# Depthwise convolution taps: from VectorE and GpSimd to VectorE and float32 products on TensorE

## The chip, the cores and the metric

The kernel runs on one core of a Trainium2 chip. The metric is the device time of one execution in microseconds; the time of a kernel is the median of its runs. The engines are named as in the profile: PE is TensorE's matrix products (PEld its weight loads), DVE is VectorE, ACT is ScalarE, POOL is GpSimd.

## The reference

Two decoder layers on 256 tokens of width 1024. In each layer one normalised input feeds two groups: attention with three branches, and a convolution module on 512 channels. Their outputs go through one output projection; a dense (layer 0) or a routed (layer 1) channel mixer follows. The convolution module is what the change is about:

```python
CONV_WIDTH = D_MODEL // 2      # 512 channels
CONV_KERNEL = 31               # taps
...
def conformer_conv(u, conv_w, conv_b, ln_g, ln_b):
    a, g = jnp.split(u, 2, axis=-1)
    h = a * jax.nn.sigmoid(g)
    h = jnp.pad(h, ((0, 0), (CONV_KERNEL - 1, 0), (0, 0)))
    y = lax.conv_general_dilated(h, conv_w[:, None, :], window_strides=(1,), padding='VALID',
                                 dimension_numbers=('NWC', 'WIO', 'NWC'),
                                 feature_group_count=CONV_WIDTH)
    y = y + conv_b
    return jax.nn.silu(layer_norm(y, ln_g, ln_b))
```

Each channel has its own 31 weights, so the convolution is 31 shifted copies of `h`, each times one number per channel, summed.

## The kernel before

Weights stream from memory in tiles of 1 MB; each half tile is split into two float32r parts, `wh` on ScalarE (line 189) and `wl` on VectorE (line 190), and each product with weights is three float32r products (`mm3`, lines 275 to 277). Inside a layer's attention phase nothing is scheduled by a planner: the string `SEQ` is a list of unit names, and the program issues the units in that order. Each engine runs its own instructions strictly in that order and waits at an instruction until what it needs from other engines is there.

The convolution is channel-major: four chunks of 128 channels (two *pairs* of chunks), 256 tokens along a row. The units that matter here:

- `uA` and `uB` are the input projections of pair 0 and pair 1, 16 units each, six products of 256 columns a unit. After the last unit of a pair, `glu` writes the gated input of the pair to `hpad` (ScalarE `th`, VectorE `hpad`).
- `v` is one tap of one chunk on VectorE (`tap_v`, line 593): `cv = cv + hpad shifted * weight`, 128 x 256. The first 17 taps of pair 0 and 16 of pair 1 go this way (`NDT`), 66 units a layer.
- `g` is one tap of one chunk in two steps (`tap_g`): ScalarE multiplies (`tap`, line 602), GpSimd adds to `cvg` (line 603). These are the other 14 and 15 taps, 58 units a layer.
- `S0` to `S11` are the score steps of attention: products into `pss` (lines 699 and 702), then VectorE's row minimum `nm` (line 704), then ScalarE's exponentials `sc` (line 707). `P0` to `P11` transpose a step's exponentials on TensorE (`ptp`, line 844) and copy them out on ScalarE (`prT`, line 846). `V0` to `V11` are the float32 products with the values (`po`, line 859).
- `ph0` to `ph3` are float32 products of 31 columns for the compressed branch (line 774), `gelu`, `heads`, `cnorm` and `keys` what follows on them; `cs`, `cp`, `cv0`, `cv1` are the compressed branch's scores (`psc`, line 867, then `scmp` on VectorE and `pcmp` on ScalarE), probabilities and values.
- `lm0` and `lm1` add `cvg` to `cv` (line 925), `lmean` begins the layer norm over channels with float32 products `pmean` of 256 columns (line 930).

The accumulation tiles of two banks each (`acc_bank`) rotate over two buffers: `pkv`, `pu` of pair 0, `pu` of pair 1, `po` of both token blocks, `pout`.

Of the kernel before, what the change touches and what calls it, by code (L numbers as in the profile page):

```python
# [47 lines left out]
NDT = (17, 16)  # L48
NPT = (0, 0)
SEQ = """  # L50
    qr0 kv kv qs1 qr1 kv kv kv kv qx1 kv kv qs0 ks1 kvc kvc kvc kvc kvc kvc qt11 kr0 kr1 ks0 kvc kvc uA uA uA
    setup uA uA gt gt gt kx0 uA uA uA kx1 gt qx0 uA uA uA kt10 uA uA uA uA uA v kvo gt kt00 v gt v g v g g g v v v
    v g v swap blk1 g v blk0 uB g g v gt uB v v g v uB g kt01 kt11 uB uB g gt v uB qt10 g uB v uB v g v gtan v g v
    uB uB v uB v g g v v v qt00 g uB qt01 g g uB g g g S0 ph0 g v uB ph1 gate v g v g v S1 v v v ph2 uB v v uB g
    P0 ph3 v g P1 gelu v g S2 heads v g g g v g P2 S3 S4 cnorm V0 g v v V1 v keys v g S5 v g P3 cs0 v g g v V2 g
    P4 S6 P5 v v v g V3 S7 v cs1 g g v cp0 g g S8 g v V4 P6 g g P7 g g join0 S9 cv0 cp1 v V5 v g g V6 v turn0 g g
    v v v lm0 g V7 oa g P8 g g P9 S10 S11 g V8 v v oa P10 g P11 v v v v V9 v V10 v v lm1 V11 join1 lmean cv1 oa
# [12 lines left out]
def trunk(ctx: ExitStack, tc: tile.TileContext, x, positions, attn_norm_g, ffn_norm_g, w_in, w_out,  # L70
# [28 lines left out]
    # ------------------------------------------------------------------ the stream of weights  # L99
# [49 lines left out]
    class Stream:  # L149
        """Weight tiles in the order of use: loads run RAW tiles ahead, the split into two  # L150
        float32r parts runs WB - 1 half tiles ahead."""
# [21 lines left out]
        def whole(self):  # L173
            """the next tile that is used as it is, and its number"""
            n = self.order[1].pop(0)
            return n, self.raws[n]
# [29 lines left out]
        def take_group(self, n):  # L206
            """n parts of one half tile each that are used more than once: no half tile beyond
            the buffers is split before their use"""
            return [self.take(WB - j) for j in range(n)]
# [9 lines left out]
    # ------------------------------------------------------------------ first loads  # L219
# [17 lines left out]
    # ------------------------------------------------------------------ constants  # L237
# [100 lines left out]
    def boundary(key, nrm, tails, heads, banks, **more):  # L338
        """the end of one part and the start of the next, with the norm between them; the order is
        that of the letters: o, a unit of the end (the last four those of the second token block);  # L340
        h, a unit of the start for the first block; z y x and a q u t, the norm of the two blocks;
        m, half a weight tile to split"""
# [7 lines left out]
    # ------------------------------------------------------------------ rest of the setup  # L350
# [103 lines left out]
    def rope(sm, v, cs, sn):  # L454
        """v [n, heads, 64]; the first 16 of the last axis rotated in place"""
# [11 lines left out]
    # ================================================================== layers  # L467
    for layer in range(DEPTH):
# [16 lines left out]
        # ---- queries, token-major  # L485
# [70 lines left out]
        # ---- inputs of the convolution, channel-major: two chunks of 128 channels at a time  # L556
# [18 lines left out]
        cvg = nsm.tile([P, D], F32, name="cvg", tag="xn").rearrange("p (c t) -> p c t", c=4)  # L575
# [9 lines left out]
        # causal depthwise conv, tap by tap beside other work: the first taps of a chunk on VectorE,  # L585
        # some on TensorE, the others multiplied on ScalarE and summed on GpSimd
# [9 lines left out]
        def tap_g(c, j, first):  # L596
            src = hpad[:, c, j:j + S]
            if first:
                nc.scalar.activation(cvg[:, c], src, AF.Copy, scale=cw5[layer][:, c, j:j + 1])
            else:  # L600
                tap = sm.tile([P, S], F32, name="tap", bufs=3)
                nc.scalar.activation(tap, src, AF.Copy, scale=cw5[layer][:, c, j:j + 1])  # L602
                nc.gpsimd.tensor_tensor(cvg[:, c], cvg[:, c], tap, op=ALU.add)  # L603

        pcv = {}

        def tap_p(pair, j, first, last):
            """a tap of two chunks on TensorE, by diagonal matrices"""
            cs_ = slice(2 * pair, 2 * pair + 2)
            if first:  # L610
                pcv[pair] = bank_a("pcv").rearrange("p (c t) -> p c t", c=2)
            dg = sm.tile([P, 2, P], F32, name="dg", tag="tap", bufs=3)
            nc.gpsimd.tensor_tensor(dg, ident[:, None, :].to_broadcast([P, 2, P]),
                                    cw5[layer][:, cs_, j:j + 1].to_broadcast([P, 2, P]), op=ALU.mult)
            for c in range(2):
                nc.tensor.matmul(pcv[pair][:, c], dg[:, c], hpad[:, 2 * pair + c, j:j + S],
                                 start=(first and c == 0), stop=last, skip_group_check=True)

        vs, gs, ps = [], [], []
        for pair in range(2):  # L620
            nd = NDT[pair]
            ng = nd + NPT[pair]
            vs.append([lambda c=c, j=j: tap_v(c, j) for j in range(nd) for c in (2 * pair, 2 * pair + 1)])
            ps.append([lambda pair=pair, j=j, nd=nd, ng=ng: tap_p(pair, j, j == nd, j == ng - 1)
                       for j in range(nd, ng)])
            gs.append([lambda c=c, j=j, ng=ng: tap_g(c, j, j == ng) for j in range(ng, CONV_K)
                       for c in (2 * pair, 2 * pair + 1)])

        def some(lst, n):
            for _ in range(n):  # L630
                for pair in sorted(ready):
                    if lst[pair]:
                        lst[pair].pop(0)()
                        break
# [6 lines left out]
        # ---- keys and values of the causal branches: token-major  # L641
# [41 lines left out]
        # ---- attention: the two causal branches, 512 score columns a step; the steps of both  # L683
        # token blocks form one pipeline
# [26 lines left out]
        # ---- inputs of the compressed branch and gates, channel-major  # L711
# [50 lines left out]
        # ---- compressed keys and values  # L762
# [74 lines left out]
        # ---- the steps of attention after the scores  # L837
# [79 lines left out]
        # ---- layer norm of the conv over channels and swish  # L917
        ln = {}

        def ln_merge(pair):  # L920
            c = slice(2 * pair, 2 * pair + 2)
            if NPT[pair]:
                nc.vector.tensor_tensor(cv[:, c], cv[:, c], pcv[pair], op=ALU.add)
            if NDT[pair] + NPT[pair] < CONV_K:
                nc.vector.tensor_tensor(cv[:, c], cv[:, c], cvg[:, c], op=ALU.add)
# [44 lines left out]
        # ---- output projection  # L970
# [17 lines left out]
        def out_conv(k, b):  # L988
            if b == 0 and k == 0:
# [11 lines left out]
                 "p": [lambda: some(ps, 1)] * (2 * CONV_K),  # L1001
                 "v": [lambda: some(vs, 1)] * (4 * CONV_K), "g": [lambda: some(gs, 1)] * (4 * CONV_K),
# [21 lines left out]
        events += [("lm0", lambda: ln_merge(0)), ("lm1", lambda: ln_merge(1)), ("lmean", ln_mean), ("lvar", ln_var), ("lscale", ln_scale), ("lout", ln_out)]  # L1024
# [6 lines left out]
        for name in SEQ.split():  # L1031
            units[name].pop(0)()
        phase.close()

        # ---- channel mixer
# [5 lines left out]
        # the scale of the tokens is left out where the experts apply it  # L1041
# [9 lines left out]
        def logits(b):  # L1051
            """the router's logits of a token block, channel-major"""
# [14 lines left out]
        if layer % 2 == 0:  # L1067
# [44 lines left out]
            def ffn_first():  # L1112
                """the first columns, token-major: the first token block starts before the second"""
# [70 lines left out]
        # ---- routed experts  # L1184
# [10 lines left out]
        # rank of each logit in its row; equal logits rank by index  # L1195
# [12 lines left out]
        # slot of each token within its expert: tokens before it that chose the same expert  # L1208
# [24 lines left out]
        def gather(pair, banks):  # L1233
            """the tokens of a pair of experts, channel-major; in units of 256 channels and one part"""
# [33 lines left out]
        def of_slots(dst, ps, e, src):  # L1268
            """a value of each token, for the tokens in the slots of an expert"""
# [271 lines left out]
```

## Time and profile before

| | |
|---|---|
| time, median of 3 runs | 1623.56 us (1615.91 to 1625.65) |
| span of the profiled execution, first to last instruction | 1617.5 us |
| PE busy over the span | 1546.0 us (96%) |
| DVE busy | 1342.1 us (83%) |
| ACT busy | 1093.4 us (68%) |
| POOL busy | 126.0 us (8%) |
| mean granted TensorE clock | 0.971 |

The span is the only time that the profiled execution has of itself; it lies 6 us under the median of the runs and inside their range. A granted clock of 1.0 is 2.4 GHz, 0.5 is 1.2 GHz; a mean between them is a share of both. Busy shares are averages over the program: the attention phase of layer 0 takes roughly the first 160 us, that of layer 1 lies between 412 and 560 us, and in the rest of the time the mixers run with PE over 90% busy and GpSimd idle. Durations of single instructions overlap with those of their neighbours, so a row that merges several (x7) gives the better price of one.

### The profile page before, as it was taken

What the parts mean: (1) busy time and instruction counts of PE and PEld (TensorE: products, weight loads), DVE (VectorE), ACT (ScalarE), POOL (GpSimd) and SP (SyncE); (2) the same over time, 40 slices, a digit from 0 to 9 for tenths busy, and PEclk for the clock granted to TensorE, in tenths of its full rate; (3) what the DMA queues carried; (4) which work ended last, traced back from release to release, by engine and by line L of the source; (5) the groups of instructions that cost most, each with busy time, mean ns of one, the idle gap of its engine ahead of it and who ended that gap; (6) DMA issues with size and microseconds to landing.
All of it is one profiled execution on the core that took longest, in us unless ns stands there. A gap on an engine that the chain in (4) does not pass through costs nothing.

```text
span 1617.5 us, 21390 instructions
## 1 busy us (share of the span) xinstructions
PE 1546.0 (96%) x7861; PEld 1294.0 (80%) x7861; DVE 1342.1 (83%) x1647; ACT 1093.4 (68%) x1430; POOL 126.0 (8%) x152
## 2 busy tenths in 40 slices
PE   6989999999997989999999999999999999999997
PEld 5977899999796768878877877887877877878785
DVE  7898655554789889989989989989989989998995
ACT  5765544444466568777877877777877777777774
POOL 2453000000155200000000000000000000000000
PEclk9978999999997999999999999999999999999998
DMA  9700585546632249999999998999999999998990
GB/s 307 223 27 1 187 304 182 183 167 198 158 105 79 79 151 373 378 323 335 362 336 337 371 337 314 359 349 338 371 339 330 338 353 329 367 369 314 362 364 27
DMA packets 197744, 433.75 MB, mean 268 GB/s; under 512 B 10346, under 2 KB 28978, under 8 KB 197636
## 3 DMA queue, kind: packets, MB, share of 16 engines
q1 hardware_dynamic: 196902, 432.02, 75.6%
q8 instruction: 63, 1.03, 0.3%
q0 software_dynamic: 288, 0.30, 0.1%
q14 instruction: 45, 0.37, 0.1%
q10 hardware_dynamic: 446, 0.03, 0.0%
HBM read 431.27 MB, written 1.05 MB: 267 GB/s over the span
## 4 chain that ended last, share of the span: by engine, by line
PE 77%; DVE 17%; ACT 3%; issue 2%; DMA 1%; POOL 0%; SPq 0%; DVEq 0%; ACTq 0%
PE pg L275 12%; PE pg L277 12%; PE pg L276 12%; PE pd L277 7%; PE pd L276 7%; PE pd L275 7%; DVE wl L190 5%; DVE cv L593 4%; PE pgu L275 3%; PE pgu L277 3%; PE pgu L276 3%; PE pt L288 2%; ACT wh L189 1%; PE pgx L1243 1%; DVE xt L1404 1%
## 5 line engine op out<-in xcount | busy, mean ns | idle before, releaser
L190 DVE TENSOR_TENSOR wl<-raw,wh 128x1024 fp32r<-128x1024 f32 x808 | 981.3, 1227 | 189.3 <-ACT wh L189 164.7
L189 ACT CAST wh<-raw 128x1024 fp32r<-128x1024 f32 x808 | 845.9, 1052 | 326.7 <-PE pg L277 126.4
L275 PE MATMUL pg<-wh,xgH 128*128 128x512 f32 x896 | 353.8, 395 | 6.5 <-DVE xt L1404 6.5
L277 PE MATMUL pg<-wh,xgL 128*128 128x512 f32 x896 | 353.5, 394 | 0.0
L276 PE MATMUL pg<-wl,xgH 128*128 128x512 f32 x896 | 352.5, 393 | 0.0
L275 PE MATMUL pd<-wh,fh 128*128 128x512 f32 x560 | 226.5, 404 | 0.1
L276 PE MATMUL pd<-wl,fh 128*128 128x512 f32 x560 | 222.2, 397 | 1.3 <-DVE wl L190 1.3
L277 PE MATMUL pd<-wh,fl 128*128 128x512 f32 x560 | 222.9, 398 | 0.0
L275 PEld LDWEIGHTS pg<-wh,xgH 128*128 128x128 f32 x896 | 170.3, 190 | 43.8 <-ACT wh L189 9.3
L277 PEld LDWEIGHTS pg<-wh,xgL 128*128 128x128 f32 x896 | 169.9, 190 | 36.5 <-DVE xgL L1247 0.5
L276 PEld LDWEIGHTS pg<-wl,xgH 128*128 128x128 f32 x896 | 170.5, 190 | 35.8 <-DVE wl L190 0.3
L276 PEld LDWEIGHTS pd<-wl,fh 128*128 128x128 f32 x560 | 105.8, 189 | 24.9 <-DVE wl L190 2.0
L277 PEld LDWEIGHTS pd<-wh,fl 128*128 128x128 f32 x560 | 105.6, 189 | 25.1 <-DVE fl L272 0.2
L275 PEld LDWEIGHTS pd<-wh,fh 128*128 128x128 f32 x560 | 105.9, 189 | 22.8 <-ACT fh L271 0.3
L275 PE MATMUL pgu<-hFH,wh 128*128 128x256 f32 x384 | 108.9, 284 | 0.8 <-DVE posT L452 0.8
L277 PE MATMUL pgu<-hFH,wl 128*128 128x256 f32 x384 | 108.7, 283 | 0.0
L276 PE MATMUL pgu<-hFL,wh 128*128 128x256 f32 x384 | 108.7, 283 | 0.0
L603 POOL TENSOR_TENSOR cvg<-cvg,tap 128x256 f32<-128x256 f32 x108 | 97.4, 929 | 75.4 <-ACT tap L602 71.9
L275 PEld LDWEIGHTS pgu<-hFH,wh 128*128 128x128 f32 x384 | 73.7, 192 | 1.1 <-PE pgk L1080 0.9
L276 PEld LDWEIGHTS pgu<-hFL,wh 128*128 128x128 f32 x384 | 73.7, 192 | 0.2
L277 PEld LDWEIGHTS pgu<-hFH,wl 128*128 128x128 f32 x384 | 73.7, 192 | 0.0
L593 DVE SCALAR_TENSOR_TENSOR cv<-hpad,cw,cv 128x256 f32<-128x256 f32 x124 | 72.2, 635 | 0.0
(371 smaller groups left out, 1655.1 us busy)
## 6 DMA issues: line engine op xcount, KB each, us to landing
raw<-in_moe_w_gate_dram SPq DMA_DIRECT2D x112, 1024.0 KB, 5.5
raw<-in_moe_w_up_dram SPq DMA_DIRECT2D x112, 1024.0 KB, 5.7
raw<-in_moe_w_down_dram SPq DMA_DIRECT2D x112, 1024.0 KB, 5.1
raw<-in_w_in_dram SPq DMA_DIRECT2D x18, 1024.0 KB, 9.5
raw<-in_ffn_w_gate_dram SPq DMA_DIRECT2D x14, 1024.0 KB, 7.9
raw<-in_ffn_w_up_dram SPq DMA_DIRECT2D x14, 1024.0 KB, 5.1
raw<-in_ffn_w_down_dram SPq DMA_DIRECT2D x14, 1024.0 KB, 4.9
raw<-in_w_out_dram SPq DMA_DIRECT2D x8, 1024.0 KB, 10.6
```

The source lines that it names most:

```text
L189: nc.scalar.copy(h, r)
L190: nc.vector.tensor_tensor(lo, r, h.bitcast(F32), op=ALU.subtract)
L275: nc.tensor.matmul(dst, ah, bh, start=start, stop=False, skip_group_check=skip)
L276: nc.tensor.matmul(dst, ah, bl, start=False, stop=False, skip_group_check=skip)
L277: nc.tensor.matmul(dst, al, bh, start=False, stop=stop, skip_group_check=skip)
L288: nc.tensor.transpose(pt[:, k], src[:, k * P:(k + 1) * P], ident)
L593: nc.vector.scalar_tensor_tensor(cv[:, c], src, cw5[layer][:, c, j:j + 1], cv[:, c], op0=ALU.mult, op1=ALU.add)
L603: nc.gpsimd.tensor_tensor(cvg[:, c], cvg[:, c], tap, op=ALU.add)
L1243: nc.tensor.matmul(pgx, src[:, b, k * P:(k + 1) * P], ohs[pair][:, b].rearrange("p e s -> p (e s)"), start=(m == 0 and b == 0), stop=(m == ...
L1404: nc.vector.tensor_tensor(xt[:, b, ns], xt[:, b, ns], pc, op=ALU.add)
```

## The change

`NDT` becomes 19 for both pairs. The other 12 taps of a chunk are made on TensorE, by a unit `p`: for one tap of one pair, ScalarE writes two diagonal matrices `dg` (the identity, 128 x 128, times the tap's weights as scale), and TensorE multiplies each as float32 with the shifted `hpad` (128 x 256) into `pcv`, an accumulation tile of two banks from `acc_bank`. There are 24 units `p` a layer, 48 products, with three buffers for `dg`. All `g` units are gone, with `cvg`; GpSimd has no part in the convolution. `lp0` and `lp1` add `pcv` to `cv` and stand right after `cs1`; further `v` units follow them. `SEQ` is rewritten accordingly. The core of the diff (blanked comments are left out):

```diff
-NDT = (17, 16)
-NPT = (0, 0)
+NDT = (19, 19)
 SEQ = """
     qr0 kv kv qs1 qr1 kv kv kv kv qx1 kv kv qs0 ks1 kvc kvc kvc kvc kvc kvc qt11 kr0 kr1 ks0 kvc kvc uA uA uA
-    setup uA uA gt gt gt kx0 uA uA uA kx1 gt qx0 uA uA uA kt10 uA uA uA uA uA v kvo gt kt00 v gt v g v g g g v v v
-    v g v swap blk1 g v blk0 uB g g v gt uB v v g v uB g kt01 kt11 uB uB g gt v uB qt10 g uB v uB v g v gtan v g v
-    uB uB v uB v g g v v v qt00 g uB qt01 g g uB g g g S0 ph0 g v uB ph1 gate v g v g v S1 v v v ph2 uB v v uB g
-    P0 ph3 v g P1 gelu v g S2 heads v g g g v g P2 S3 S4 cnorm V0 g v v V1 v keys v g S5 v g P3 cs0 v g g v V2 g
-    P4 S6 P5 v v v g V3 S7 v cs1 g g v cp0 g g S8 g v V4 P6 g g P7 g g join0 S9 cv0 cp1 v V5 v g g V6 v turn0 g g
-    v v v lm0 g V7 oa g P8 g g P9 S10 S11 g V8 v v oa P10 g P11 v v v v V9 v V10 v v lm1 V11 join1 lmean cv1 oa
+    setup uA uA gt gt gt kx0 uA uA uA kx1 gt qx0 uA uA uA kt10 uA uA uA uA uA v kvo gt kt00 v gt v v v v v
+    v swap blk1 v v blk0 uB gt uB v v v v uB kt01 kt11 uB uB v gt v uB qt10 v uB v uB v v gtan v v
+    uB uB v uB v v v v v qt00 uB qt01 p uB p S0 ph0 p v v uB ph1 gate p v p v S1 p v v v ph2 uB p v v uB
+    p P0 ph3 v p v P1 gelu p v S2 heads p v v p v P2 p S3 p S4 p cnorm V0 p v v V1 p v keys p v S5 v p P3 p cs0 v p v V2
+    P4 p S6 P5 v v v p V3 p S7 v cs1 lp0 lp1 cp0 S8 v V4 P6 v P7 join0 S9 cv0 cp1 v V5 v v V6 v turn0
+    v v v v v v V7 oa v P8 P9 S10 S11 V8 v v oa P10 P11 v v v v V9 v V10 v v V11 join1 lmean cv1 oa
     lvar turn1 lscale oa oa lout oa oa oa
 """
...
-        cvg = nsm.tile([P, D], F32, name="cvg", tag="xn").rearrange("p (c t) -> p c t", c=4)
...
-        def tap_g(c, j, first):
-            src = hpad[:, c, j:j + S]
-            if first:
-                nc.scalar.activation(cvg[:, c], src, AF.Copy, scale=cw5[layer][:, c, j:j + 1])
-            else:
-                tap = sm.tile([P, S], F32, name="tap", bufs=3)
-                nc.scalar.activation(tap, src, AF.Copy, scale=cw5[layer][:, c, j:j + 1])
-                nc.gpsimd.tensor_tensor(cvg[:, c], cvg[:, c], tap, op=ALU.add)
-
...
+        def tap_p(pair, j):
+            if not pcv:
+                pcv["p"] = acc_bank("pcv").rearrange("p a (c t) -> p a c t", c=2)
+            dg = sm.tile([P, 2, P], F32, name="dg", bufs=3)
             for c in range(2):
+                nc.scalar.activation(dg[:, c], ident, AF.Copy, scale=cw5[layer][:, 2 * pair + c, j:j + 1])
+            for c in range(2):
+                nc.tensor.matmul(pcv["p"][:, pair, c], dg[:, c], hpad[:, 2 * pair + c, j:j + S],
+                                 start=(j == NDT[pair] and c == 0), stop=(j == CONV_K - 1), skip_group_check=True)
...
-            if NPT[pair]:
-                nc.vector.tensor_tensor(cv[:, c], cv[:, c], pcv[pair], op=ALU.add)
-            if NDT[pair] + NPT[pair] < CONV_K:
-                nc.vector.tensor_tensor(cv[:, c], cv[:, c], cvg[:, c], op=ALU.add)
+            assert not ps[pair]
+            nc.vector.tensor_tensor(cv[:, c], cv[:, c], pcv["p"][:, pair], op=ALU.add)
```

On TensorE the score steps S3 and S4 of layer 0 and the first value products stood in a row before (`pss` S3, `pss` S4, `po` V0 and V1, `pkc` the keys, `pss` S5); line numbers are those of the kernel before:

```order
L844 MATMUL ptp<-ident,sc_1155 128x128 x4
L699 MATMUL pss<-kT,qT 128x256 x4
L702 MATMUL pss<-cmask,identR 128x512
L699 MATMUL pss<-kT,qT 128x512 x2
L702 MATMUL pss<-cmask,identR 128x2x128
L859 MATMUL po<-v_sb,prT 128x64 x8
L833 MATMUL pkc<-ident,kcd 128x16 x2
L699 MATMUL pss<-kT,qT 128x512 x2
```

The same place on TensorE in the changed kernel, whose lines 825, 680, 683 and 840 are the transposes, the two score lines and the value products, and whose line 604 is the new product:

```order
L825 MATMUL ptp<-ident,sc_1129 128x128 x4
L604 MATMUL pcv<-hpad,dg 128x256 x2
L680 MATMUL pss<-kT,qT 128x256 x4
L683 MATMUL pss<-cmask,identR 128x512
L604 MATMUL pcv<-hpad,dg 128x256 x2
L680 MATMUL pss<-kT,qT 128x512 x2
L683 MATMUL pss<-cmask,identR 128x2x128
L604 MATMUL pcv<-hpad,dg 128x256 x2
L840 MATMUL po<-v_sb,prT 128x64 x4
L604 MATMUL pcv<-hpad,dg 128x256 x2
```

A unit `p`, two products, now stands between the transposes and S3, between S3 and S4, and behind S4.

On ScalarE the same place before, where `sc` are the exponentials of S3 and of S4, `tap` and `cvg` the multiplied taps, and `prT` the copy of P2:

```order
L602 ACTIVATE tap<-hpad,cw_604 128x256 [waits Pool_49] x2
L846 COPY prT<-ptp 128x512 [waits PE_49]
L707 ACTIVATE sc_1202,rsum<-pss,nm 128x128 [waits DVE_49]
L707 ACTIVATE sc_1202,rsum<-pss,nm 128x128 x3
L707 ACTIVATE sc_1215,rsum<-pss,nm 128x256 [waits DVE_49]
L707 ACTIVATE sc_1215,rsum<-pss,nm 128x256
L602 ACTIVATE tap<-hpad,cw_604 128x256 [waits Pool_49]
```

And on ScalarE in the changed kernel, whose lines 827, 688 and 602 are the copy, the exponentials and the diagonal matrices:

```order
L827 COPY prT<-ptp 128x512 [waits PE_49]
L602 ACTIVATE dg<-ident,cw_603 128x128 [waits Activation_49]
L602 ACTIVATE dg<-ident,cw_603 128x128
L688 ACTIVATE sc_1184,rsum<-pss,nm 128x128 [waits DVE_49]
L688 ACTIVATE sc_1184,rsum<-pss,nm 128x128 x3
L602 ACTIVATE dg<-ident,cw_603 128x128 [waits Activation_49]
L602 ACTIVATE dg<-ident,cw_603 128x128
L688 ACTIVATE sc_1202,rsum<-pss,nm 128x256 [waits DVE_49]
L688 ACTIVATE sc_1202,rsum<-pss,nm 128x256
L602 ACTIVATE dg<-ident,cw_603 128x128 [waits Activation_49]
```

The two `dg` of a unit `p` stand behind the exponentials of the score step that precedes the unit, and these wait for VectorE's `nm` of that step.

## Rows read from the trace of the kernel before

**Rows 1.** Busy time by engine in four stretches, us; (x) counts instructions; then granted clock, DMA.
```profile
62.60:75.10 12.50, 12.38 (x101) 11.81 (x101) 12.39 (x24) 10.31 (x23) 10.05 (x11) 1.00 0.25 76
75.10:112.95 37.85, 33.81 (x194) 30.62 (x193) 35.32 (x76) 23.66 (x78) 21.16 (x25) 0.68 0.16 55
112.95:140.20 27.25, 23.55 (x138) 19.93 (x137) 26.66 (x52) 20.01 (x57) 18.26 (x23) 0.87 0.01 1
475.48:513.56 38.08, 30.84 (x194) 27.47 (x192) 35.61 (x75) 24.91 (x79) 21.08 (x25) 0.78 0.32 110
```

**Rows 2.** VectorE in order of time, layer 0: start, us, instruction, count.
```profile
63.21 2.86 DVE L593 SCALAR_TENSOR_TENSOR cv<-hpad,cw,cv 128x256 f32<-128x256 f32 x7
...
78.71 5.29 DVE L593 SCALAR_TENSOR_TENSOR cv<-hpad,cw,cv 128x256 f32<-128x256 f32 x6
...
88.70 0.68 DVE L704 TENSOR_REDUCE nm<-pss 128x4 f32<-128x512 f32 x1
...
104.13 0.69 DVE L704 TENSOR_REDUCE nm<-pss 128x4 f32<-128x512 f32 x1 [0.74 <-PE pss L702]
...
109.91 0.27 DVE L869 TENSOR_TENSOR scmp<-psc,cmpm 128x128 f32<-128x128 f32 x1
...
111.07 1.35 DVE L593 SCALAR_TENSOR_TENSOR cv<-hpad,cw,cv 128x256 f32<-128x256 f32 x2
...
115.18 0.68 DVE L704 TENSOR_REDUCE nm<-pss 128x2 f32<-128x512 f32 x1
```

**Rows 3.** VectorE by line and shape, 62 to 148 us: busy us, mean ns, idle before.
```profile
L593 DVE SCALAR_TENSOR_TENSOR cv<-hpad,cw,cv 128x256 f32<-128x256 f32 x62 | 36.0, 634 | 0.0
L190 DVE TENSOR_TENSOR wl<-raw,wh 128x1024 fp32r<-128x1024 f32 x5 | 7.1, 1429 | 0.0
...
L925 DVE TENSOR_TENSOR cv<-cv,cvg 128x512 f32<-128x512 f32 x2 | 1.9, 956 | 0.1
```

**Rows 4.** TensorE in order of time, layer 0.
```profile
77.10 0.74 PE L699 MATMUL pss<-kT,qT 128*128 128x256 f32 x4 [1.04 <-ACT qT L554]
...
77.90 1.86 PE L774 MATMUL ph<-blk,raw 128*128 128x31 f32 x16
...
79.81 0.28 PE L276 MATMUL pu<-hTL,wh 128*128 128x256 f32 x1
79.93 0.28 PE L277 MATMUL pu<-hTH,wl 128*128 128x256 f32 x1
...
108.29 0.60 PE L844 MATMUL ptp<-ident,sc 128*128 128x128 f32 x4
...
112.14 1.00 PE L859 MATMUL po<-v_sb,prT 128*128 128x64 f32 x8
112.95 0.71 PE L699 MATMUL pss<-kT,qT 128*128 128x512 f32 x2
113.50 0.28 PE L702 MATMUL pss<-cmask,identR 128*128 128x256 f32 x1
```

**Rows 5.** TensorE, 139.1 to 139.9 us: two float32 products of 256 columns, two rows each.
```profile
139.16 1.08 PE L930 MATMUL pmean<-cv,ones 128*128 128x256 f32 x4
```

**Rows 6.** ScalarE in order of time, layer 0.
```profile
104.86 0.37 ACT L707 ACTIVATE sc<-pss,nm 128x128 f32<-128x128 f32 x1 [0.51 <-DVE nm L704]
...
106.24 0.48 ACT L707 ACTIVATE sc<-pss,nm 128x256 f32<-128x256 f32 x1
...
107.14 0.53 ACT L602 ACTIVATE tap<-hpad,cw 128x256 f32<-128x256 f32 x1
...
110.93 0.58 ACT L846 COPY prT<-ptp 128x512 f32<-128x512 f32 x1
111.40 0.33 ACT L875 ACTIVATE pcmp<-scmp 128x128 f32<-128x128 f32 x1
```

**Rows 7.** TensorE, a wait for ScalarE (in brackets: idle before, what ended it).
```profile
121.72 1.13 PE L894 MATMUL poc<-vblk,pcT 128*128 128x512 f32 x2 [1.63 <-ACT prT L846]
```

**Rows 8.** The slice of 10 us after that wait, columns as in Rows 1.
```profile
120.00:130.00 10.00, 8.22 (x35) 7.11 (x35) 9.72 (x20) 8.27 (x23) 8.13 (x11) 0.66 0.00 0
```

More of the change, by code (lines that the diff above doesn't have):

```diff
@@ L605, in trunk @@
-        pcv = {}
[L607 to L614, printed above, removed]
-            for c in range(2):
-                nc.tensor.matmul(pcv[pair][:, c], dg[:, c], hpad[:, 2 * pair + c, j:j + S],
-                                 start=(first and c == 0), stop=last, skip_group_check=True)
@@ L619, in trunk @@
[L619 to L634, printed above, removed]
+        pcv = {}
+        def tap_p(pair, j):
+            if not pcv:
+                pcv["p"] = acc_bank("pcv").rearrange("p a (c t) -> p a c t", c=2)
+            dg = sm.tile([P, 2, P], F32, name="dg", bufs=3)
+            for c in range(2):
+                nc.scalar.activation(dg[:, c], ident, AF.Copy, scale=cw5[layer][:, 2 * pair + c, j:j + 1])
+            for c in range(2):
+                nc.tensor.matmul(pcv["p"][:, pair, c], dg[:, c], hpad[:, 2 * pair + c, j:j + S],
+                                 start=(j == NDT[pair] and c == 0), stop=(j == CONV_K - 1), skip_group_check=True)
@@ L636, in trunk, with some @@
+        vs = [[lambda c=c, j=j: tap_v(c, j) for j in range(NDT[pair]) for c in (2 * pair, 2 * pair + 1)]
+              for pair in range(2)]
+        ps = [[lambda pair=pair, j=j: tap_p(pair, j) for j in range(NDT[pair], CONV_K)] for pair in range(2)]
+        def some(lst):
+            for pair in sorted(ready):
+                if lst[pair]:
+                    lst[pair].pop(0)()
+                    break
         w1 = {}
@@ L1000, in trunk @@
                  "oc": [lambda k=k, b=b: out_conv(k, b) for b in range(NB) for k in range(4)],
-                 "p": [lambda: some(ps, 1)] * (2 * CONV_K),
-                 "v": [lambda: some(vs, 1)] * (4 * CONV_K), "g": [lambda: some(gs, 1)] * (4 * CONV_K),
+                 "p": [lambda: some(ps)] * (2 * CONV_K), "v": [lambda: some(vs)] * (4 * CONV_K),
                  "setup": [lambda: layer or setup_layer(0)]}
@@ L1023, in trunk @@
         events += [("gelu", cmp_gelu), ("heads", cmp_heads), ("cnorm", cmp_norm), ("keys", cmp_keys)]
-        events += [("lm0", lambda: ln_merge(0)), ("lm1", lambda: ln_merge(1)), ("lmean", ln_mean), ("lvar", ln_var), ("lscale", ln_scale), ("lout", ln_out)]
+        events += [("lp0", lambda: ln_merge(0)), ("lp1", lambda: ln_merge(1)), ("lmean", ln_mean), ("lvar", ln_var), ("lscale", ln_scale), ("lout", ln_out)]
         for b in range(NB):
@@ L1032, in trunk @@
             units[name].pop(0)()
+        assert not any(vs + ps)
         phase.close()
```

## Prediction

> **What bounds the kernel now.** I read the busy times of the whole program first: PE is at 96%, so the mixers cannot gain from this change; they hold no convolution. The change lies in two attention phases, so I cut that of layer 0 at three points that both kernels pass: the end of `uA` (62.6 us), the last query transpose `qt01` (75.1 us), the products of S7 (112.95 us), and the start of the last layer norm products (140.2 us) [rows 1]. In the first stretch PE is busy all the time with `uB`; nothing that VectorE is spared there shows. In the second, the **stretch** below, 37.85 us, VectorE is busy 35.32 us and PE 33.81 us, but PE at a granted clock of 0.68, so its work is less than its busy time says. In the third VectorE is busy 26.66 of 27.25 us. Layer 1 has the same stretch, 38.08 us.
>
> Then VectorE in order of time [rows 2]. Seven taps alone take 2.86 us, 0.41 each; six taps while GpSimd adds take 5.29 us, 0.88 each. Over the phase 62 of them take 36.0 us, 0.58 each [rows 3]. VectorE falls behind: S0's products were issued from 77.10 us and done before the next at 77.90 us [rows 4], yet its `nm` runs at 88.70 us [rows 2]. So VectorE sets the pace today, slowed by GpSimd.
>
> **What is removed.** 58 multiplications on ScalarE and their additions on GpSimd go, with the contention. 66 taps at 0.58 were 38.3 us; 76 at 0.41 are 31.2 us, so VectorE gains 7 us a layer although it has ten more taps. ScalarE's trade costs nothing by itself: it was busy 23.66 of 37.85 us [rows 1].
>
> **What TensorE gets.** All 24 units `p` stand between `qt01` and S7. A float32 product of 256 columns has a near row: two of `pmean` take 1.08 us in four rows [rows 5]; a modelled end lies some 0.16 us behind the next start (0.28 us long, 0.12 apart, `pu` in rows 4), so 0.92 us for two, 0.46 each. 48 of them are 22.1 us a layer. Bounds: 0.43 and 0.54 each (without the start-up; without taking the end off), 20.6 to 25.9 us.
>
> PE's own work in the stretch at full clock [rows 4]: 24 `uB` products, 0.12 apart, 2.9; four `ph` at 1.86, 7.4; S0 to S3 at 0.80 (77.10 to 77.90), 3.2; S4 to S6 at 0.67, 2.0; six P at 0.45 (0.60 less its end), 2.7; four V at 0.81 (112.14 to 112.95), 3.2; the small ones (`cs0`, heads, gate, keys), an estimate, 1.6. That is 23.0 us. With the new products 45.1 us, more than the 37.85 us that the stretch lasts now. PE is the floor there whatever else happens.
>
> **The wait that the order adds.** ScalarE works in order, and the `dg` of a unit stand behind whatever ScalarE does for the unit ahead. Behind a score step that is: PE's end 0.16, `nm` 0.69 (104.13 to 104.82) and hand-over 0.04 [rows 2], four exponentials with their sums 1.38 (104.86 to 106.24) [rows 6], then `dg`. A 128x128 scale by a column has no row; the nearest is the exponential of that size with a bias column, 0.37, and a 128x256 `tap` is 0.53 [rows 6], so 0.37 to 0.53; I take 0.40 with the hand-over. Together 2.7 us from S0 to S3, and 2.2 us for the later steps, whose exponentials take 0.90 (106.24 to 107.14). PE waits all that time where `p` follows the step at once, and whatever PE has next (the other steps, `ph`, V) queues behind it. Before, a step was followed by other products, and its exponentials were needed much later. The list, from the order of the units:
> - S0: 2.7 less `ph0` 1.86, 0.8. S1: 2.7. S2: 2.7 less the heads' small products, some 0.6 as for four transposes [rows 4], 2.1. S3: 2.7. S4, S5, S6: 2.2 each, 6.6.
> - P2, P3, P4: copy `prT` 0.58 [rows 6], `dg`, PE's end, 1.1 each, 3.3.
> - `cs0`: `scmp` on VectorE from 109.91 to 111.07 [rows 2], `pcmp` 0.33 [rows 6], `dg`, 2.0.
> - four more places (behind the query copy, GLU's tanh, gelu, the keys' copy), one ScalarE instruction and `dg` each, taken like a P, 4.4.
>
> Sum 24.6 us. Bounds: a third less where work overlaps, 16; nothing hides more, since `dg` has three buffers but cannot pass the exponentials in ScalarE's queue. That PE waits like this for ScalarE's queue is seen today: 1.63 us before `poc`, behind a `prT` [rows 7].
>
> Stretch: 23.0 + 22.1 + 24.6 = 69.7 us against 37.85, **+31.9 us** a layer. VectorE's 25 taps and other work there fit beside it.
>
> **Behind S7.** 18 taps at 0.58 become 23 at 0.41, -1.0; the merge of `cvg` was once hindered (two take 1.9 us, 0.69 alone would do [rows 3]), -0.5; VectorE starts S7's `nm` at 115.18 us, though its products end at 113.78 [rows 2, 4], -1.4 when it is no longer behind. -2.9 us, bounds 0 and -6.
>
> **The clock.** Today the slice after PE's waits around 120 us has a granted clock of 0.66 [rows 8], and the stretch has 0.68 and 0.78 [rows 1]. The new stretch has waits of over 2 us eight times, but dense products between them. At 0.87, between today's and full clock, 45.1 us of work cost 6.7 us more; I take +7. Bounds 0, and at 0.68, +21.
>
> Other edits cost nothing: `pcv` takes its buffer after `glu` of pair 0 has read it, long before; V4 needs it back after `lp1`, a few VectorE instructions behind S7, in a part that VectorE sets; the stream of weights has its buffers filled (DMA 0.16 busy).
>
> **Sum.** 31.9 - 2.9 + 7 = 36 us a layer, 72 us in both. The profiled span of 1617.5 us becomes 1689.5; it lies 6 us under the median, so the median of 1623.56 becomes **1695 us**. Own range: 1660 (waits 8 less, -6 behind S7, full clock: 18 a layer) to 1730 (clock at 0.68, nothing behind S7: 53 a layer).
>
> **Rivals.**
> 1. *PE as the floor, no waits.* If ScalarE runs far enough ahead, the stretch is 45.1 us: +7.3 - 2.9, 9 us in both layers, **1632**. For it: PE has to do this work anyway; against it: ScalarE's order, in which no `dg` precedes the exponentials of the step ahead of it.
> 2. *Faster: VectorE's relief is all that counts.* VectorE sets two of three stretches [rows 1] and gains 7.2 us of taps and 0.5 at the merge a layer, 15 us in all, **1608**. It decides only if the 48 products fit into 37.85 - 7.7 - 23.0 = 7 us, 0.15 us each; rows 5 say 0.46. The Trainium skill bears on this (SBUF — State Buffer, "Who interferes with whom"): a VectorE instruction with two SBUF inputs and a GpSimd one that reads SBUF exclude each other for a whole instruction. By that rule, the trace agrees: 0.88 against 0.41 us; the rule gives this rival its gain, but says nothing of PE.
> 3. *The clock stays low.* If the waits hold PE at half clock through the stretch, its 45.1 us take up to 90: 31.9 - 2.9 + 40, and allowing nothing back, 138 us in both, **1762**. For it: 0.68 today with fewer waits; against it: the products are dense, and the third stretch, with waits of its own, has 0.87 today [rows 1]. The Trainium skill warns of it (TensorE: Matmul & The Clock Gate, "Loop structure matters more than you think"): a loop that makes the matrix unit wait between products runs them cold. The trace has both, 0.66 after a wait [rows 8] and 1.00 in dense `uB` [rows 1]; by the rule taken whole the time is this rival's, by the rows it is the +7 above.
>
> That the change would not do what it says is excluded by the order of the instructions.
>
> **How the numbers follow.** The forecast has 0.80, rival 1 0.09, rival 2 0.06, rival 3 0.05. The forecast's own range leaves 0.20 out; I widen it down to 1640 for waits that overlap more than listed. Within 1% (16 us, about what a measurement here can tell from no change): rival 1 and part of rival 2, 0.12; faster 0.04; slower 0.84.
>
> **What would show it.** In the new profile: `cv` taps at 0.41 to 0.48 us with none near 0.88; pairs of `pcv` rows 0.22 to 0.25 us apart at full clock; PE idle in the stretch about 25 us, mostly ended by ScalarE's `dg`; S7 some 32 us later than `qt01`'s 37.85; VectorE idle there for the first time, waiting for `pss`. The forecast is wrong if `dg` is found ready at most units (then rival 1), or if the granted clock is near 0.5 (rival 3).

## The result, and the profile after

The changed kernel takes 1717.1 us (median of 4 runs, 1713.9 to 1720.5) against 1624.3 us for the kernel before, run beside it: ratio 1.0581, 95% interval 1.0551 to 1.0611. It is slower by 93 us, where 72 were forecast. The profiled executions differ by 95.7 us of span (1617.5 and 1713.2). One is not quite comparable with the other: a time is some 2 us longer than its span, so the profiled execution of before lies 5 us under its median and that of after 2 us.

The page of the changed kernel, busy time by engine, and its group of the new products (busy, mean ns of one | idle before them):

```profile
PE 1602.7 (94%) x8053; PEld 1340.1 (78%) x8053; DVE 1316.8 (77%) x1667; ACT 1077.6 (63%) x1410; POOL 28.3 (2%) x44
...
L604 PE MATMUL pcv<-hpad,dg 128*128 128x256 f32 x192 | 70.9, 509 | 51.9 <-ACT dg L602 49.8
```

GpSimd is out of the convolution, TensorE is busy 57 us longer (part of that is a lower clock, as will be seen), and in front of the new products it sat idle for 51.9 us, nearly all of it until ScalarE had written a `dg`. About half of that belongs to each layer. The same stretches as in [rows 1], cut at the same points (`qt01` to the products of S7 in layer 0 and in layer 1, then from S7 to the last `pmean`):

```profile
74.66:166.32 91.66, 66.24 (x290) 55.76 (x289) 28.34 (x76) 29.40 (x105) 0.69 (x1) 0.76 0.04 13
525.11:616.04 90.93, 64.47 (x290) 54.23 (x289) 28.33 (x76) 30.68 (x106) 0.69 (x1) 0.76 0.11 36
166.32:190.90 24.58, 20.28 (x137) 17.02 (x136) 22.62 (x57) 10.24 (x31) 0.00 (x0) 1.00 0.00 1
```

The stretch takes 91.66 us instead of 37.85, and 90.93 instead of 38.08: +53.8 and +52.9 us. TensorE is busy 66.24 us of it and idle 25.4; VectorE, busy 35.32 us there before, now is busy 28.34 us of 91.66. Behind S7 the part that took 27.25 us takes 24.58 (in layer 1, to the start of the first `pmean`, 25.2 instead of 26.6). Together that is +103 us up to `pmean` in both layers; 1.2 us a layer come back between `pmean` and the last product of the output projection (29.7 us before and 28.5 after, in layer 0), and 4 us in the mixer of layer 1; why, I did not follow.

TensorE in order of time at the place that the orders ahead of the prediction show (P2, S3, S4, V0; in brackets the idle time before a row and what ended it):

```profile
122.65 1.13 PE L604 MATMUL pcv<-hpad,dg 128*128 128x256 f32 x4 [0.97 <-ACT dg L602]
123.43 0.82 PE L680 MATMUL pss<-kT,qT 128*128 128x256 f32 x4
124.09 0.39 PE L683 MATMUL pss<-cmask,identR 128*128 128x512 f32 x1
127.08 1.13 PE L604 MATMUL pcv<-hpad,dg 128*128 128x256 f32 x4 [2.61 <-ACT dg L602]
127.86 0.82 PE L680 MATMUL pss<-kT,qT 128*128 128x512 f32 x2
128.52 0.28 PE L683 MATMUL pss<-cmask,identR 128*128 128x256 f32 x1
130.92 1.13 PE L604 MATMUL pcv<-hpad,dg 128*128 128x256 f32 x4 [2.12 <-ACT dg L602]
```

VectorE and ScalarE at that step, in order of time:

```profile
124.51 0.69 DVE L685 TENSOR_REDUCE nm<-pss 128x4 f32<-128x512 f32 x1 [5.62 <-PE pss L683]
...
125.24 0.37 ACT L688 ACTIVATE sc<-pss,nm 128x128 f32<-128x128 f32 x1 [2.35 <-DVE nm L685]
...
126.62 0.70 ACT L602 ACTIVATE dg<-ident,cw 128x128 f32<-128x128 f32 x2
```

Read them as one circle, that of S3. The products of S3 end at 124.48 us (124.09 + 0.39), `nm` runs from 124.51, the exponentials from 125.24, the two `dg` only from 126.62, since they stand behind the exponentials in ScalarE's order, and the new products from 127.08. Then S4 may start, and the circle begins anew. While TensorE waits VectorE and ScalarE have little else: VectorE had been idle 5.62 us before this `nm`, ScalarE 2.35 us before the exponentials. Nothing is full; three engines hand one step round.

VectorE by line and shape, 62 to 192 us, answering to [rows 3]:

```profile
L591 DVE SCALAR_TENSOR_TENSOR cv<-hpad,cw,cv 128x256 f32<-128x256 f32 x72 | 30.2, 477 | 0.0
...
L685 DVE TENSOR_REDUCE nm<-pss 128x2 f32<-128x512 f32 x8 | 5.4, 687 | 19.6 <-PE pss L683 19.6
L685 DVE TENSOR_REDUCE nm<-pss 128x4 f32<-128x512 f32 x4 | 2.8, 690 | 10.4 <-PE pss L683 10.4
...
L904 DVE TENSOR_TENSOR cv<-cv,pcv 128x512 f32<-128x512 f32 x2 | 1.3, 680 | 0.0
```

A tap takes 0.42 us in the mean (30.2 / 72) instead of 0.58, the merge 0.65 instead of 0.95, and VectorE is idle 30 us in front of the `nm` steps; before, such a wait was 0.74 us at S3 [rows 2].

Two slices of the stretch, columns as in [rows 1]:

```profile
120.00:130.00 10.00, 5.21 (x22) 3.63 (x21) 1.83 (x4) 3.70 (x15) 0.00 (x0) 0.91 0.00 0
...
150.00:160.00 10.00, 8.12 (x27) 6.56 (x27) 1.42 (x4) 2.07 (x6) 0.00 (x0) 0.53 0.00 0
```

The slice with the most idle time has a granted clock of 0.91, and one that is busy 8.12 of 10 us has 0.53, nearly all of it at 1.2 GHz. So TensorE seems to pay for the waits twice: while it waits, and in work elsewhere that then runs at the lower clock. How much each is, the trace alone does not say.

One more wait is new, behind S7: V4 waits 2.08 us for the merge of `pcv` (line 904), whose accumulation tile it needs.

```profile
170.89 1.08 PE L840 MATMUL po<-v_sb,prT 128*128 128x64 f32 x8 [2.08 <-DVE cv L904]
```

### The profile page after: what moved, and what is told of

Same layout as the page of the kernel before. It is cut to its first block, busy times and chain, and to the rows that moved or that the text cites. A ratio compares the mean times of both kernels' runs of the same rounds, so it can differ in the third digit from the quotient of the medians.

```text
span 1713.2 us, 21573 instructions
## 1 busy us (share of the span) xinstructions
PE 1602.7 (94%) x8053; PEld 1340.1 (78%) x8053; DVE 1316.8 (77%) x1667; ACT 1077.6 (63%) x1410; POOL 28.3 (2%) x44
## 4 chain that ended last, share of the span: by engine, by line
PE 82%; DVE 10%; ACT 4%; issue 2%; DMA 1%; POOL 0%; SPq 0%; DVEq 0%; ACTq 0%
PE pg L274 11%; PE pg L276 11%; PE pg L275 11%; PE pd L276 7%; PE pd L275 7%; PE pd L274 7%; PE pcv L604 4%; DVE wl L189 3%; PE pgu L274 3%; PE pgu L276 3%; PE pgu L275 3%; PE pt L287 2%; DVE cv L591 1%; PE po L840 1%; ACT wh L188 1%
## 5 line engine op out<-in xcount | busy, mean ns | idle before, releaser
L604 PE MATMUL pcv<-hpad,dg 128*128 128x256 f32 x192 | 70.9, 509 | 51.9 <-ACT dg L602 49.8
L604 PEld LDWEIGHTS pcv<-hpad,dg 128*128 128x128 f32 x192 | 42.5, 243 | 65.1 <-ACT dg L602 57.3
```

Of the source, the lines that this page charges most:

```text
L604: nc.tensor.matmul(pcv["p"][:, pair, c], dg[:, c], hpad[:, 2 * pair + c, j:j + S], start=(j == NDT[pair] and c == 0), stop=(j == CONV_K - ...
```

## The experiments

The theory to be tested: the change costs what ScalarE's order makes TensorE wait, and what the lower clock after the waits costs; TensorE's work by itself, 45 us in the stretch with the added products, costs next to nothing more than VectorE needed before. The rivals: it is the float32 products themselves; or a shortage of buffers; or the time lies behind S7. One correction: the first expectations speak of a stretch of 93.3 us, which was read to the products of S8; to those of S7 it is 91.7.

### 1. The diagonal matrices written two units ahead

Products, their places and the three buffers stay; only ScalarE's instructions move. The first unit `p` writes the `dg` of three units, each later one those of the unit two further on.

```diff
+        dgs, todo = {}, [(pair, j) for pair in range(2) for j in range(NDT[pair], CONV_K)]
...
-            dg = sm.tile([P, 2, P], F32, name="dg", bufs=3)
-            for c in range(2):
-                nc.scalar.activation(dg[:, c], ident, AF.Copy, scale=cw5[layer][:, 2 * pair + c, j:j + 1])
+            n = (pair, j) == (0, NDT[0])
+            for _ in range(min(3 if n else 1, len(todo))):
+                q, i = todo.pop(0)
+                dg = dgs[q, i] = sm.tile([P, 2, P], F32, name="dg", bufs=3)
+                for c in range(2):
+                    nc.scalar.activation(dg[:, c], ident, AF.Copy, scale=cw5[layer][:, 2 * q + c, i:i + 1])
+            dg = dgs.pop((pair, j))
```

> The diagonal matrices of a unit p are written two units earlier in ScalarE's order; the products, their places on TensorE and everything else stay. In the changed kernel the stretch from the last query transpose to S7 lasts 93.3 us in layer 0 (37.85 before), of which TensorE waits 25.4 us, nearly all of it for a dg. My theory (waits for dg behind the exponentials, and through them the clock): the waits go, TensorE's work stands without gaps, so the clock comes back too: stretch 45 to 55 us, time 1717 - 2 x 38 to 48, so 1621 to 1641 us. Rival (the products and the clock set it, the waits are a by-product): the stretch loses at most the 25 us of waits and stays at 65 us or more, 1660 us or more. A second rival (the products are short of something else, so that the waits move to another place): over 1690 us.

Measured: 1623.1 us, ratio to the kernel before 0.9997 (0.9985 to 1.0009). The two stretches of layer 0, `qt01` to S7 and from S7:

```profile
74.85:119.89 45.04, 44.02 (x290) 39.91 (x289) 28.30 (x76) 29.10 (x105) 0.69 (x1) 1.00 0.08 27
119.89:144.00 24.11, 21.09 (x135) 17.54 (x134) 22.13 (x56) 10.25 (x31) 0.00 (x0) 0.93 0.00 1
```

The whole loss of 94 us is gone with one change of order on ScalarE, and neither buffers nor the products can have caused it. The same 290 rows of TensorE are busy 44.02 us at a clock of 1.00 instead of 66.24 at 0.76, and of the 25.4 us of idle time 1.02 is left. The stretch is 45.04 us, where the prediction summed 45.1 us of work for TensorE.

### 2. Waits filled with products that add zeros

To part the waits from the clock: in the changed kernel 47 more float32 products a layer, of the identity with a column of zeros, run on TensorE ahead of the units that wait. They change no result; `dg` stays where the change put it.

```diff
+FILL = {2: 5, 5: 5, 7: 3, 9: 2, 10: 4, 12: 2, 13: 5, 14: 4, 17: 1, 18: 4, 19: 2, 20: 4, 21: 2, 22: 4}
...
+            for _ in range(FILL.get(12 * pair + j - NDT[pair], 0)):
+                nc.tensor.matmul(pcv["p"][:, 0, 0], ident, hpad[:, 0, 0:1].to_broadcast([P, S]),
+                                 start=False, stop=False, skip_group_check=True)
```

> As the changed kernel, but ahead of the units p that wait for a dg TensorE makes 1 to 5 extra float32 products (the identity times columns of zeros, added to pcv, 0.46 us each at full clock, 47 a layer, so 21 us of work that fits into the waits). Nothing waits less. My theory of the clock (the waits turn the clock down, and the work between them then costs some 20 us a layer more): with the waits filled the granted clock of the stretch rises from 0.76 to 0.95 or more and the time falls although TensorE does more: stretch 72 to 78 us, 1677 to 1687 us. Rival (the clock costs little, the products are dearer than counted): the stretch stays at 93 us or grows by the part of the extra products that doesn't fit, 1717 to 1740 us.

Measured: 1680.7 us, ratio 1.0358 (1.0341 to 1.0375). The stretch of layer 0, two slices of it, and a run of five fillers:

```profile
74.93:147.65 72.72, 68.12 (x384) 56.61 (x383) 28.34 (x76) 29.40 (x105) 0.69 (x1) 1.00 0.05 17
...
100.00:110.00 10.00, 9.63 (x60) 7.83 (x59) 5.06 (x19) 4.37 (x17) 0.69 (x1) 1.00 0.00 0
...
130.00:140.00 10.00, 9.36 (x53) 7.52 (x52) 1.95 (x6) 3.39 (x13) 0.00 (x0) 1.00 0.00 1
...
115.06 2.34 PE L605 MATMUL pcv<-hpad,ident 128*128 128x256 f32 x10
```

More work makes the kernel 36 us faster, as expected. With the clock at 1.00 throughout, the stretch is 72.7 us, so of the 46.6 us by which the changed kernel's stretch (91.66) exceeds that of experiment 1 (45.04), the clock is 18.9 and the waits 27.7. From the windows alone the parting is 22.2 (busy 66.24 against 44.02) and 24.4 (idle 25.4 against 1.02). The two ways differ by 3 us, perhaps because a filler can outlast its wait; the clock's part lies between 19 and 22 us a layer. The five fillers take 2.34 us, less the 0.16 us of a modelled end 0.44 us each.

### 3. All taps on VectorE

No unit `p`, no GpSimd; each `p` of the sequence becomes two `v`.

```diff
-NDT = (19, 19)
+NDT = (31, 31)
...
-uB uB v uB v v v v v qt00 uB qt01 p uB p S0 ph0 p v v uB ph1 gate p v p v S1
+uB uB v uB v v v v v qt00 uB qt01 v v uB v v S0 ph0 v v v v uB ph1 gate v v v v v v S1
```

> All 31 taps on VectorE (124 units v a layer, each unit p replaced by two v), none on TensorE, none on GpSimd. It does the one half of the change alone: GpSimd leaves. VectorE's taps cost 124 x 0.41 = 50.8 us a layer where they were 38.3 us. If VectorE sets the phase, as I read the profile before, this is 8 to 12 us a layer more, 1640 to 1650 us. Rival (the contention with GpSimd costs more than the taps that GpSimd takes over): 1624 us or less.

Measured: 1624.7 us, ratio 1.0011 (1.0000 to 1.0022). My expectation was 15 us too high; the rival's bound was missed by 0.7 us. The stretch of layer 0 with two slices, and the taps by line, 62 to 148 us:

```profile
75.64:120.58 44.94, 37.70 (x195) 34.71 (x193) 43.52 (x118) 13.48 (x52) 0.69 (x1) 0.58 0.08 26
...
70.00:80.00 10.00, 10.00 (x88) 9.96 (x87) 9.99 (x21) 4.03 (x6) 0.00 (x0) 1.00 0.35 110
80.00:90.00 10.00, 10.00 (x60) 9.88 (x60) 9.96 (x25) 2.11 (x12) 0.00 (x0) 0.66 0.28 102
```

```profile
L584 DVE SCALAR_TENSOR_TENSOR cv<-hpad,cw,cv 128x256 f32<-128x256 f32 x120 | 49.6, 476 | 0.0
```

VectorE is full (43.52 of 44.94 us) and sets the pace. But 120 taps now take 49.6 us, 0.41 each, where 62 took 36.0 us beside GpSimd [rows 3]: 58 more for 13.6 us. So of the 24 us that 58 taps take at 0.41, GpSimd's units in the kernel before spared VectorE 13.6 and cost it 10 in its other taps; in the time of the kernel they bought nothing.

TensorE's clock is 0.58 here, and its waits do not explain where it falls: between 80 and 90 us, where TensorE has been busy without a gap since 70 us. Its first wait comes at 92 us. So the clock can fall without a wait too; what makes it fall there was not tried.

### 4. The changed kernel without its products

The 12 taps of TensorE, `dg` and both merges are left out.

```diff
-        ps = [[lambda pair=pair, j=j: tap_p(pair, j) for j in range(NDT[pair], CONV_K)] for pair in range(2)]
+        ps = [[], []]
...
-uB uB v uB v v v v v qt00 uB qt01 p uB p S0 ph0 p v v uB ph1 gate p v p v S1
+uB uB v uB v v v v v qt00 uB qt01 uB S0 ph0 v v uB ph1 gate v v S1
```

> As the changed kernel with the units p, the dg and the merges left out: 12 of the 31 taps of each channel are missing. It prices VectorE's relief alone, rival 2 of the prediction. By my sums VectorE gains 7 to 8 us a layer: 1606 to 1611 us. If VectorE was not what set the phase, 1618 us or more; if the relief is larger than counted (TensorE's clock comes back when VectorE no longer holds it up), 1600 us or less.

Measured: 1595.1 us, ratio 0.9825 (0.9808 to 0.9841): 28 us below the kernel before where some 15 were expected, and in the range named for a clock that comes back. The stretch, and the slice of 80 to 90 us:

```profile
74.69:108.90 34.21, 31.46 (x195) 29.32 (x193) 27.90 (x76) 14.87 (x57) 0.69 (x1) 0.75 0.10 35
...
80.00:90.00 10.00, 8.45 (x70) 7.89 (x69) 9.06 (x26) 5.00 (x21) 0.00 (x0) 1.00 0.22 84
```

It is 34.21 us, 3.6 less than before. From `qt01` to the first `pmean` layer 0 gains 7.4 us (56.6 instead of 64.1) and layer 1 10.8; 3 us more are gained behind `pmean` in both, 3 in the mixers, and the last 4 are the distance of the profiled execution of before from its median. The relief is so about twice what rival 2 counted, though the clock did not come back: it is 0.75 in this stretch (0.68 before) and 0.73 in that of layer 1 (0.78 before). In the slice that had 0.66 in experiment 3 it is 1.00, with the same products in the same order and more idle time.

What the 24 units cost when their waits are gone is the difference to experiment 1, 28 us for 96 products, 0.29 us each. That is less than a product takes, and not because it fits beside something else: TensorE is idle only 2.75 us in this stretch. But its 195 rows are busy 31.46 us at 0.75, and in experiment 1, at 1.00, 44.02 us less 48 products of 0.44 leave 22.9 us for the same work. The added products thus came with a higher clock, which pays for about 9 of their 21 us in the stretch of layer 0.

### 5. Taps moved from behind S7 into the stretch

In experiment 1 VectorE is busy 28.30 of 45.04 us in the stretch and 22.13 of 24.11 behind it, so 13 of its 23 taps behind S7 were moved ahead of it (the expectation counts 10), everything else as in experiment 1.

```diff
-P4 p S6 P5 v v v p V3 p S7 v cs1 lp0 lp1 cp0 S8 v V4 P6 v P7 join0 S9 cv0 cp1 v V5 v v V6 v turn0
-v v v v v v V7 oa v P8 P9 S10 S11 V8 v v oa P10 P11 v v v v V9 v V10 v v V11 join1 lmean cv1 oa
+P4 p v S6 P5 v v v p V3 p v S7 cs1 lp0 lp1 cp0 S8 V4 P6 P7 join0 S9 cv0 cp1 V5 V6 v turn0
+v v V7 oa v P8 P9 S10 S11 V8 v oa P10 P11 v v V9 v V10 v v V11 join1 lmean cv1 oa
```

> As e1_dg_ahead, with 10 of VectorE's taps moved from behind S7 into the stretch ahead of it, where VectorE was busy 28.3 of 45.0 us there; behind S7 it was busy 22.1 of 24.1 us. My theory (TensorE sets the stretch, VectorE what follows): the part behind S7 falls by up to 10 x 0.41 = 4 us a layer, 1615 to 1619 us against 1623. Rival (the moved taps delay the row minima, and TensorE waits for these in the stretch): 1623 us or more.

Measured: 1623.4 us, ratio 0.9999 (0.9984 to 1.0015), no gain. Behind S7, 125 to 140 us, first experiment 1, then this one:

```profile
125.00:140.00 15.00, 14.10 (x85) 11.50 (x84) 14.72 (x35) 7.04 (x20) 0.00 (x0) 0.89 0.01 1
```

```profile
125.00:140.00 15.00, 15.00 (x94) 12.55 (x95) 13.43 (x32) 8.07 (x24) 0.00 (x0) 0.89 0.00 1
```

With VectorE relieved TensorE is busy all the 15 us, at the same clock of 0.89. Two engines were close to full there, and the relief of one is worth only the distance to the other: from S7 to `pmean` 1.8 us are gained (120.54 to 142.50 against 119.89 to 143.62), of which the longer stretch takes 0.5 back; the 1.3 us a layer that would remain are about what these runs can tell from nothing. That VectorE alone set this part was wrong.

### 6. Fewer products: 23 taps on VectorE, 8 on TensorE

Experiment 1 with 16 units `p` instead of 24, and eight more taps of VectorE for each pair of chunks. In its order 20 taps more than in experiment 1 stand in the stretch and 4 fewer behind S7, where one unit `p` now stands too.

```diff
-NDT = (19, 19)
+NDT = (23, 23)
...
-uB uB v uB v v v v v qt00 uB qt01 p uB p S0 ph0 p v v uB ph1 gate p v p v S1
+uB uB v uB v v v v v qt00 uB qt01 p uB S0 ph0 v v v p uB ph1 gate v v v p S1
```

> As e1_dg_ahead, with 23 taps on VectorE and 8 on TensorE (16 units p a layer), and VectorE's taps spread as in e5_taps_earlier. 16 products fewer are 7.4 us less in the stretch at 0.46 us, 16 taps more are 6.6 us for VectorE, of which it has room. If the split of the taps is what matters (balance between the two engines): 1600 to 1611 us. If VectorE sets the phase again, and with it the clock falls: 1615 us or more.

Measured: 1610.0 us, ratio 0.9919 (0.9901 to 0.9937), faster than both kernels. The stretch:

```profile
75.05:113.91 38.86, 37.31 (x255) 33.18 (x253) 35.60 (x96) 24.19 (x89) 0.69 (x1) 1.00 0.09 31
```

TensorE is busy 37.31 and VectorE 35.60 of 38.86 us, both nearly full, at a clock of 1.00.

### 7. The kernel before without GpSimd's additions

ScalarE's multiplications stay; the additions to `cvg`, that is all but the first of a chunk's 14 or 15 taps there, are left out.

```diff
                 nc.scalar.activation(tap, src, AF.Copy, scale=cw5[layer][:, c, j:j + 1])
-                nc.gpsimd.tensor_tensor(cvg[:, c], cvg[:, c], tap, op=ALU.add)
```

> The kernel before with GpSimd's additions left out (ScalarE still multiplies): 13 and 14 of the 31 taps are missing, apart from that all stays. It prices GpSimd's contention by itself. By my sums VectorE gains 66 x 0.17 = 11 us a layer on the taps, of which only what lies behind the TensorE-bound first stretch shows, 7 to 9 us: 1605 to 1610 us. Rival (the contention is paid mostly where VectorE isn't late): 1618 us or more. If the relief also brings TensorE's clock back: 1600 us or less.

Measured: 1591.6 us, ratio 0.9800 (0.9770 to 0.9829). Lower than either theory said but for the case that named the clock. The stretch of layer 0 and that of layer 1, and VectorE's taps, 62 to 130 us:

```profile
74.94:102.75 27.81, 25.97 (x195) 23.85 (x193) 24.96 (x70) 21.45 (x74) 0.69 (x1) 0.94 0.13 44
458.80:495.60 36.80, 34.92 (x195) 32.72 (x193) 25.85 (x71) 24.07 (x78) 0.69 (x1) 0.68 0.28 89
```

```profile
L593 DVE SCALAR_TENSOR_TENSOR cv<-hpad,cw,cv 128x256 f32<-128x256 f32 x62 | 26.1, 475 | 0.0
```

The same 62 taps take 26.1 us instead of 36.0 [rows 3], and the stretch of layer 0 is 10 us shorter (27.81 against 37.85) at a clock of 0.94 instead of 0.68. That of layer 1 is only 1.3 us shorter (36.80 against 38.08), at a clock of 0.68 instead of 0.78, with TensorE busy 34.92 us of it. So the additions on an engine that was 8% busy cost the kernel 32 us, 10 us a layer of it in VectorE's taps. TensorE's clock moved up in one layer and down in the other; that VectorE's relief moves it is not shown.

### 8. Still fewer: 26 taps on VectorE, 5 on TensorE

Made like experiment 6, with 10 units `p`: nine more taps of VectorE in the stretch, three more behind it.

```diff
-NDT = (19, 19)
+NDT = (26, 26)
...
-uB uB v uB v v v v v qt00 uB qt01 p uB p S0 ph0 p v v uB ph1 gate p v p v S1
+uB uB v uB v v v v v qt00 uB qt01 p uB S0 ph0 v v v uB ph1 gate v v v v S1
```

> 26 taps on VectorE, 5 per pair on TensorE (10 units p), diagonal matrices two units ahead; nine taps more than with 23 stand in the stretch and three behind S7. With 23 taps VectorE was busy 35.7 of 39 us in the stretch and TensorE 37.5, both nearly full. Theory (VectorE is the next bound): nine taps of 0.41 us make VectorE's work there 39.3 us, the stretch 40 to 42 us, and 1.2 us more behind S7, so 1612 to 1619, slower than 23 taps. Rival (TensorE still sets the pace): six products pairs fewer are 5.5 us less in a stretch, and the time is 1599 to 1605. A granted clock under 0.9 in the stretch would say that TensorE waits for VectorE again, as with all taps on VectorE (1625).

Measured: 1615.7 us, ratio 0.9953 (0.9939 to 0.9967), inside the first theory's range. The stretch:

```profile
74.85:114.47 39.62, 34.52 (x231) 31.12 (x229) 37.55 (x102) 20.38 (x75) 0.69 (x1) 0.91 0.10 31
```

VectorE is now the fuller engine (37.55 of 39.62 us). TensorE is idle 5.1 us, of which the trace puts 1.5 down to VectorE (`kcd`), and its clock is down to 0.91, 0.87 in layer 1. The stretch grows by 0.8 us in layer 0 and by 2.1 in layer 1 (38.8 to 40.9), and from S7 to `pmean` it is 0.5 more in each. With `dg` ahead 19, 23 and 26 taps on VectorE give 1623, 1610 and 1616 us, and 31, without any `dg`, 1625: the best of them is the one whose two engines are most nearly equally full.

## Why the prediction came out as it did

The direction, the mechanism and the likeliest case were right, and the time lies in the range; one term was too small. Its steps, per layer:

- **TensorE's work in the stretch**, 23.0 + 22.1 = 45.1 us. Experiment 1 ran that work nearly without waits: 45.04 us. That the two agree to a tenth is luck, since 1.02 us of it is idle time ahead of the first unit. The work is 44.0 us, and the price of 0.46 us, worked out from two `pmean` rows, is a little high: fillers in a row take 0.44 each (experiment 2), which would make the sum 44.1.
- **The waits**, 24.6 us forecast. The trace has 25.4 us in fifteen places, all but the first ended by `dg`: behind P2 0.97 (1.1 forecast), behind S3 2.61 (2.7), behind S4 2.12 (2.2). One was misjudged: at S0 I took `ph0` off the wait and left 0.8, and 2.62 were measured: S0's products were done at 79.3 us, but VectorE was still at its taps and then at a weight split `wl`, and its `nm` ran only at 81.01. Most others lie up to 0.2 us under their forecast, which takes half of it back. Experiment 1 shows the cause: with the order changed and nothing else, the waits go.
- **Behind S7**, -2.9 forecast; -2.7 measured in layer 0 (27.25 to 24.58), -1.4 in layer 1. The prediction put V4's wait for the merge at nothing; it is 2.08 us in both layers, inside these differences.
- **VectorE's taps** at 0.41 and none near 0.88: 0.42 in the mean. VectorE waits for `pss`, as was said.
- **The clock**, +7 forecast with an upper bound of +21: 19 to 22 measured in experiment 2 and in the windows. This is the term that was mis-sized, by 12 to 15 us a layer. I took the granted clock at 0.87, between the old stretch and full clock, and argued that the dense products between the waits would hold it. It was 0.76 over the stretch. And even that flatters: the mean counts the idle time too, while the work itself got 44.02 / 66.24, which is 0.66. The old stretch's 0.68, which stood as the bound, was the better row to take. The rule of the Trainium skill that was weighed there (TensorE: Matmul & The Clock Gate, "Loop structure matters more than you think") is borne out by the rows of the changed kernel as to its direction (its example is a long wait for a transfer, the waits here last 0.6 to 2.6 us), though not taken whole: by rival 3, at half clock throughout, the time would have been 1762 us. (The line of rival 3, 45.1 us of work that take 90, adds 45 us a layer and not 40, which would be 1772.)

The sum: the two stretches came out 14.9 and 14.0 us longer than the 38.9 forecast (31.9 and 7), 12 to 15 of it the clock in each. With 29 for them, 2 for what follows S7, and -7 outside the parts that were counted (ahead of `qt01`, behind `pmean`, in a mixer), 72 becomes 96, the difference of the spans; that of the medians is 93, since the two profiled executions lie unequally far under theirs.

**Rival 1**, TensorE as the floor without waits, was priced at 1632 us. Experiment 1 is that rival: 1623 us. Of the 9 us that it was to be slower than the kernel before, the traces show 8.7 up to `pmean` (68.8 us from `qt01` instead of 64.1, and 68.8 instead of 64.7); 3 come back between `pmean` and the last product of the output projection, so that the spans differ by 4.5 (1617.5 and 1622.0), and the rest is the distance of the profiled execution of before from its median.

**Rival 2**, VectorE's relief, was priced at 15 us. Experiment 4 gives 28 us with all units `g` gone and VectorE's ten more taps in place, experiment 7 gives 32 with the additions alone gone. The price counted VectorE's own time. In experiment 7 layer 0 is 14.8 us shorter from `qt01` to `pmean` and layer 1 6.5, while the clock of the stretch went from 0.68 to 0.94 in the one and from 0.78 to 0.68 in the other. So the clock decides much of what the relief is worth, and what sets it where no units `p` stand is open. In experiment 4, where ScalarE's multiplications are gone too, the clock is only 0.75, and the stretch 6.4 us longer than in experiment 7 (34.21 and 27.81), though VectorE has just 6 taps more there; in layer 1 it is the other way round (31.5 and 36.8). What makes these differences was not tried.

## What to carry to other kernels

Where an engine works in order, write the operands of a product into its queue ahead of work that depends on that product's neighbours: two units ahead, with the same three buffers, was worth 94 us here. Price a wait of TensorE twice, once for itself and once for the clock that the work around it then gets (25 and 19 to 22 us a layer here), and weigh that clock by work, not by time; but do not put every low clock down to waits (experiment 3). And before an idle engine is given a share of a full one's work, try the full one alone: here VectorE without GpSimd did as well as with it. The split that gained was that with TensorE, 8 of 31 taps, 1610 us.

## What the runs showed that was not expected

- Adding 47 useless products a layer, some 21 us at 0.44 each, made the kernel 36 us faster (1717 to 1681), by nothing but the clock: the granted clock of the stretch went from 0.76 to 1.00.
- The lowest clock does not stand where the waits are: 0.91 in the slice with 4.8 us of idle time, 0.53 in one with 1.9. And without the units `p` it falls where TensorE has no gap at all (experiment 3), and one kernel has 0.94 in the stretch of layer 0 and 0.68 in that of layer 1 (experiment 7).
- GpSimd's 54 additions a layer and ScalarE's 58 multiplications gave no gain over doing the same taps on VectorE (1624.7 us against 1623.0 for the kernel before beside it), and taking the additions away brought 32 us: VectorE's taps fall from 0.58 to 0.42 us.
